# Unread products in TensorE's pauses, S5's last block in PSUM, and the place of the adaLN sums

## The chip, the cores and the metric

The kernel runs on one core of a Trainium2 chip. Five engines work side by side on the on-chip memory: TensorE (PE; its weight loads are shown apart as PEld), VectorE (DVE), ScalarE (ACT), GpSimd (POOL) and SyncE (SP), which here only issues transfers. TensorE writes into PSUM, from which the other engines read. The metric is the device time of one execution in microseconds; lower is better.

## The reference, cut to what matters

Four layers work on 256 latent and 256 context tokens of width 1024. Layer i mixes tokens by its kind (0 pooling, 1 a bidirectional S5 state-space layer with a GLU, 2 neighbourhood attention, 3 pooling again), and a gated ConvFFN follows each.

```python
for i in range(DEPTH):
    mod_lat = (cond_lat @ ada_w[i] + ada_b[i])[:, None, :]
    sh1, sc1, g1, sh2, sc2, g2 = jnp.split(mod_lat, 6, axis=-1)
    u_lat = _modulate(_rmsnorm(h_lat, norm1_g[i]), sh1, sc1)
    ...
    h_lat = h_lat + g1 * y_lat
    v_lat = _modulate(_rmsnorm(h_lat, norm2_g[i]), sh2, sc2)
    h_lat = h_lat + g2 * _conv_ffn(v_lat, ffn_w_up[i], ffn_conv_w[i], ffn_conv_b[i], ffn_w_down[i])
```

The context stream goes through the same steps with the same weights as long as a later layer reads it. In S5 each group of 16 channels drives 64 complex states in both directions:

```python
a_bar, b_bar = _s5_discretise(a_re[direction], a_im[direction], log_dt[direction], ...)
h_lat = _diag_scan(a_bar, bu, reverse)
y_lat.append(jnp.real(jnp.einsum('blgp,gcp->blgc', h_lat, c_cplx)))
# glu_out: g = gelu(y + d_skip * u); (g @ w1 + b1) * sigmoid(g @ w2 + b2)
```

## The kernel before, in words

**Products.** A large product is made of three: weights and data are each split into a high and a low part (`whi`, `wlo`; `uh`, `ul` or `ah`, `al` or `gh`, `gl`), and `mm3` adds high x high, low x high and high x low in PSUM. SP fetches a raw block of weights, ACT makes `whi` (L58), VectorE `wlo` (L159), some blocks ahead (`ahead`, `prep_hi`, `prep_lo`, `_prep`; `prep_parts` yields between the pieces of one block). Engines take their instructions in the order in which the program issues them: this order is written by hand, and waits follow from tiles and buffers.

**Norms.** `rstd` adds up the squares of all channels by products with ones (the tile `ssq`; the last channel's squares, `sq_last`, come latest), makes the inverse root on ACT and VectorE (`rsqrt`, tile `rs`) and spreads it over 128 partitions by one product with `sel` for each group of tokens (the tile `rstd`). Then `split_mod` makes q = h x gs x rstd on VectorE, `uh` on ACT and `ul` on VectorE, channel block by channel block; `up` uses them.

**PSUM.** Eight banks: four with the tag `up` (pool `psu`), two `acc` (`psa`), two others.

**ConvFFN.** `ffn(l, ...)` goes over 11 blocks f of hidden channels: `up(half, weights, k)` for k in 0 to 7, the convolution of width 3 and the gate (VectorE and ACT, tile `t`, then `ah`, `al`), and in parts the products `dn` down to the residual stream. In block 0 the two halves run interleaved, the second `lag` steps behind the first. Ahead of ConvFFN 0, `start` has already split two channel blocks and issued the turning products of S5's tables (`s5_fat`, tiles `s5fat`, copied by ACT to `s5ft`).

**adaLN.** The modulation vectors of the next layers are summed beside the ConvFFNs (`ada_vec`). Each job is (layer, first chunk, chunks, letters): "V" multiplies and adds on VectorE in one pass of 128x2048 (L55), "P" multiplies on ACT and adds on POOL (L321), "M" does the first two as "V" and the others as "P".

**S5.** Eight blocks m of channels. `v_mm` makes v in PSUM, `scan` turns v by a decaying phase (VectorE, three passes), scans it along the tokens into an SBUF tile g (`tensor_tensor_scan`), and turns back: y1 = g x cos and y2 = g (parts swapped) x sin, two passes of 128x1024 (L1530, L1531), on POOL except that the last block's y2 is on VectorE. `join` adds y2 to y1 (L1535; VectorE, for two blocks POOL). `z_mm` makes the output of a block: 32 products with the short kernel k and 64 products with c, of 64 rows each, that read y. In the last pass of the loop, m = 7, `z_mm(6)` is issued, and behind the loop `join(7)` and `z_mm(7)`; then the GLU's products follow.

## Time and profile before

| what | value |
|---|---|
| time, median of 3 runs | 1741.68 us (1740.31 to 1742.18) |
| the profiled execution's own time | 1745.49 us |
| its span | 1743.7 us |
| mean granted clock of TensorE | 0.963 of full speed |
| TensorE busy | 1642.7 us (94%) |
| VectorE busy | 1317.5 us (76%) |
| ScalarE busy | 785.2 us (45%) |
| GpSimd busy | 382.2 us (22%) |

Busy time is the time in which an engine had an instruction in work; the granted clock is what TensorE was given, 1.0 for 2.4 GHz and 0.5 for 1.2 GHz. All times that are given as points ("at 592.1") are microseconds from the span's start.

### The profile page before, as it was taken

The numbers are of one execution on the slowest core, as the hardware profiler recorded it, in microseconds if no ns is written. First come the engines' busy times: TensorE is split into PE (matmuls) and PEld (weight loads), VectorE is DVE, ScalarE is ACT, GpSimd is POOL, SyncE is SP. The second block draws the span as 40 slices with busy tenths as digits, with TensorE's granted clock in tenths as the row PEclk, the third lists the DMA queues.
The fourth block names the chain that finished last, engine by engine and source line by source line (L and its number), as shares of the span: only waits on it lengthen the run. The fifth ranks groups of instructions, "written<-read, shape, count | busy, mean of one in ns | idle before, by whom it ended". The sixth has DMA issues, their size and how long they took to land.

```text
span 1743.7 us, 26649 instructions
## 1 busy us (share of the span) xinstructions
PE 1642.7 (94%) x10482; PEld 1359.1 (78%) x10482; DVE 1317.5 (76%) x2007; ACT 785.2 (45%) x1236; POOL 382.2 (22%) x317
## 2 busy tenths in 40 slices
PE   7899999999987898899999989999999999999998
PEld 4467778777767886787878867787778999889997
DVE  6768868799749758687878688726658989678876
ACT  4533314223263242544232543436666466575553
POOL 0015355565618501000000340201220000111001
PEclk9989999999998699899999999999999999999999
DMA  9669798786869843342646555233227866545553
GB/s 381 269 201 251 246 311 261 213 236 184 252 194 391 308 169 145 138 152 104 234 175 233 203 212 191 93 119 130 95 91 253 289 212 213 213 169 174 190 181 110
DMA packets 98181, 356.88 MB, mean 205 GB/s; under 512 B 14296, under 2 KB 37368, under 8 KB 72200
## 3 DMA queue, kind: packets, MB, share of 16 engines
q1 hardware_dynamic: 93400, 334.09, 56.8%
q0 software_dynamic: 4080, 18.99, 3.0%
q8 instruction: 83, 1.36, 0.3%
q10 hardware_dynamic: 576, 2.10, 0.3%
q14 instruction: 42, 0.34, 0.1%
HBM read 324.19 MB, written 30.94 MB: 204 GB/s over the span
## 4 chain that ended last, share of the span: by engine, by line
PE 59%; DVE 17%; DMA 5%; issue 4%; ACT 4%; POOL 3%; SPq 1%; DVEq 0%; ACTq 0%; POOLq 0%
PE p L61 28%; PE dn L61 14%; DVE wlo L159 5%; PE glu L61 4%; DMA s5fl<-s5dA 4%; DVE t L55 3%; PE v L61 2%; PE k L61 2%; PE wo L61 1%; ACT whi L58 1%; PE q L61 1%; DVE s5bt L1328 1%; DVE s5vt L1327 1%; DVE h L55 1%; PE z L61 1%
## 5 line engine op out<-in xcount | busy, mean ns | idle before, releaser
L61 PE MATMUL p<-uh,whi 128*128 128x512 f32 (+1 forms) x1408 | 482.1, 342 | 17.0 <-DVE t L55 8.2
L61 PE MATMUL p<-uh,wlo 128*128 128x512 f32 (+1 forms) x1408 | 480.2, 341 | 4.7 <-DVE wlo L159 2.8
L61 PE MATMUL p<-ul,whi 128*128 128x512 f32 (+1 forms) x1408 | 480.4, 341 | 0.6 <-DVE ul L55 0.4
L159 DVE TENSOR_TENSOR wlo<-raw,whi 128x1024 fp32r<-128x1024 f32 x334 | 378.2, 1174 | 118.6 <-ACT whi L58 117.4
L58 ACT ACTIVATE whi<-raw 128x1024 fp32r<-128x1024 f32 x352 | 318.3, 952 | 260.1 <-PE dn L61 71.7
L61 PEld LDWEIGHTS p<-uh,whi 128*128 128x128 f32 x1408 | 270.0, 192 | 58.9 <-issue 16.0
L61 PEld LDWEIGHTS p<-uh,wlo 128*128 128x128 f32 x1408 | 269.9, 192 | 36.2 <-DVE wlo L159 4.5
L61 PEld LDWEIGHTS p<-ul,whi 128*128 128x128 f32 x1408 | 269.8, 192 | 31.6 <-DVE ul L55 1.7
L61 PE MATMUL dn<-ah,wlo 128*128 128x512 f32 (+1 forms) x704 | 239.9, 341 | 9.7 <-DVE wlo L159 9.7
L61 PE MATMUL dn<-ah,whi 128*128 128x512 f32 (+1 forms) x704 | 242.0, 344 | 5.4 <-ACT whi L58 2.9
L61 PE MATMUL dn<-al,whi 128*128 128x512 f32 (+1 forms) x704 | 239.0, 340 | 2.6 <-DVE al L819 2.6
L55 DVE SCALAR_TENSOR_TENSOR t<-p,conv_sb,t 128x510 f32<-128x510 f32 (+1 forms) x352 | 208.2, 612 | 25.6 <-ACT t L58 19.3
L61 PEld LDWEIGHTS dn<-ah,whi 128*128 128x128 f32 x704 | 135.0, 192 | 29.3 <-issue 10.6
L61 PEld LDWEIGHTS dn<-ah,wlo 128*128 128x128 f32 x704 | 134.8, 191 | 27.3 <-DVE wlo L159 12.1
L61 PEld LDWEIGHTS dn<-al,whi 128*128 128x128 f32 x704 | 134.8, 191 | 17.2 <-DVE al L819 3.1
L55 DVE SCALAR_TENSOR_TENSOR ads<-ada,cT_sb,ads 128x2048 f32<-128x2048 f32 (+1 forms) x69 | 140.5, 2066 | 6.6 <-DMA ada<-in_ada_dram 5.0
L58 ACT ACTIVATE t<-p,conv_sb 128x512 f32<-128x512 f32 (+1 forms) x176 | 107.6, 661 | 53.7 <-PE p L61 53.6
L321 POOL TENSOR_TENSOR ads<-ads,ada 128x2048 f32<-128x2048 f32 (+1 forms) x11 | 45.6, 4157 | 345.1 <-ACT ada L58 334.5
L55 DVE SCALAR_TENSOR_TENSOR h<-dn,mods,h 128x256 f32<-128x256 f32 x192 | 83.8, 477 | 39.8 <-PE dn L61 39.6
L58 ACT ACTIVATE t<-t 128x512 f32<-128x512 f32 (+1 forms) x88 | 45.9, 522 | 149.6 <-DVE t L55 141.0
L58 ACT ACTIVATE ah<-t 128x512 fp32r<-128x512 f32 (+1 forms) x88 | 46.0, 523 | 141.9 <-DVE t L810 132.1
L1316 POOL TENSOR_TENSOR s5ct<-s5bc,s5pw 128x512 f32<-128x512 f32 x32 | 42.7, 1333 | 223.1 <-DMA s5bc<-in_s5c_dram 146.4
(256 smaller groups left out, 2300.2 us busy)
## 6 DMA issues: line engine op xcount, KB each, us to landing
raw<-in_wup_dram SPq DMA_DIRECT2D x88, 1024.0 KB, 5.2
ada<-in_ada_dram SPq DMA_DIRECT2D x84, 1024.0 KB, 7.6
raw<-in_wdn_dram SPq DMA_DIRECT2D x32, 768.0 KB, 4.3
raw<-in_wdn_dram SPq DMA_DIRECT2D x32, 640.0 KB, 4.0
raw<-in_qkv_dram SPq DMA_DIRECT2D x12, 1024.0 KB, 4.9
ada<-in_ada_dram POOLq DMA_DIRECT2D x12, 1024.0 KB, 5.4
s5bt<-in_s5bT_dram SPq DMA_DIRECT2D x32, 256.0 KB, 6.6
s5fl<-s5dA SPq DMA_DIRECT2D x32, 256.0 KB, 7.4
```

Of the source, the lines that this page charges most:

```text
L55: return self.nc.vector.scalar_tensor_tensor(out, in0, scalar, in1, op0=op0, op1=op1, **kw)
L58: return self.nc.scalar.activation(out, in_, func, **kw)
L61: return self.nc.tensor.matmul(out, lhsT, rhs, start=start, stop=stop)
L159: self.nc.vector.tensor_sub(lo[:, s], t[:, s], hi[:, s].bitcast(F32))
L321: self.nc.gpsimd.tensor_add(y, y, t)
L1316: G.tensor_tensor(ct[:, o], *x, op=ALU.mult)
L1327: V.tensor_mul(tv, bT[:, :, ::-1], fa[:, :, 1:2].to_broadcast([P, 2, 2, 128]))
L1328: V.tensor_mul(ba, bT, fa[:, :, 0:1].to_broadcast([P, 2, 2, 128]))
```

## The change

- A new function `keep(n)` issues n fp32 products of the identity with 256 columns of `sel` into a PSUM tile of tag `up` that nobody reads. `rstd` calls it at three places: ahead of the sums of the last squares (only where `ssq` was begun early), ahead of the inverse root's use, and after the broadcast. The numbers are (1, 4, 6) in S5, (4, 3, 3) in ConvFFN 1, (1, 3, 1) in attention, (1, 3, 2) in ConvFFN 2 and in pool layer 3, (0, 3, 2) in ConvFFN 3. `start` ends with five, S5's loop has eight in its last pass: 56 in all.
- S5's last block: the scan writes over v in PSUM, and VectorE makes y2, then v x cos in place, then y1 = sum, six passes of 128x512 in all; POOL's pass and `join(7)` go. `z_mm(7)` is issued behind the eight products and ahead of `z_mm(6)`.
- ConvFFN 0: the low parts of its first weight block are issued ahead of the second channel block's split, the preparation of the next block ahead of the last splits, and the lag is 3 instead of 4.
- The sums of (2, 8, 4) in ConvFFN 1 go from "P" to "V", those of (3, 10, 2) ahead of ConvFFN 3 from "M" to "V".

```diff
@@ -609,11 +609,13 @@
         next(t)
         next(fat[3])
         uh, ul = self.new_u()
-        self.split_mod(0, 1, LC, r, uh, ul, range(2))
+        self.split_mod(0, 1, LC, r, uh, ul, range(1))
+        next(parts)
+        next(parts)
+        self.split_mod(0, 1, LC, r, uh, ul, range(1, 2))
         for g in fat[2:]:
             next(g)
-        next(parts)
-        next(parts)
+        self.keep(5)
         self.pre = r, uh, ul, parts
 
     def mod(self, l, ch, c, d):
@@ -702,7 +704,14 @@
         self.nc.vector.tensor_copy(rc, pc)
         return rc
 
-    def rstd(self, bank=0, also=lambda: None, apart=False):
+    def keep(self, n):
+
+        if n:
+            ps = self.psu.tile([P, 512], F32, tag="up", name="keep")
+            for _ in range(n):
+                self.mm(ps[:, :2 * P], self.eye, self.sel[:, :2].rearrange("p j n -> p (j n)"), True, True)
+
+    def rstd(self, bank=0, also=lambda: None, apart=False, keep=(0, 0, 0)):
         n = self.tok().stop - self.tok().start
         ng = n // P
         ps, self.ssq = self.ssq, None
@@ -711,19 +720,23 @@
             self.sq_eps(ps)
             for j in range(ng):
                 self.mm(ps[32 * j:32 * j + 32, :P], self.ones, self.sq_acc[:, j * P:(j + 1) * P], False, False)
+            self.keep(keep[0])
             for j in range(ng):
                 self.mm(ps[32 * j:32 * j + 32, :P], self.ones, self.sq_last[:, j * P:(j + 1) * P], False, True)
         np_ = 32 * ng
+        self.keep(keep[1])
         x = self.rsqrt(ps, np_)
         also()
         if apart:
             rs = [self.psa.tile([P, T], F32, tag="acc", name="rstd"), self.bank("rstd", [P, T], bank)]
             for j in range(ng):
                 self.mm(rs[j // 2][:, j % 2 * P:(j % 2 + 1) * P], self.sel[:np_, j], x, True, True)
+            self.keep(keep[2])
             return lambda c: rs[c]
         rb = self.rb_all = self.bank("rstd", i=bank)
         for j in range(ng):
             self.mm(rb[:, j * P:(j + 1) * P], self.sel[:np_, j], x, True, True)
+        self.keep(keep[2])
         base = self.tok().start
         return lambda c: rb[:, c * T - base:(c + 1) * T - base]
 
@@ -768,7 +781,7 @@
         if len(conds) == 1:
             self.third = ap_, self.n_prep + 1, self.n_use + NF + 16
         if l:
-            r = self.r or self.rstd(apart=full)
+            r = self.r or self.rstd(apart=full, keep=(4, 3, 3) if full else (1, 3, 2))
             self.r = None
             if self.n_prep == self.n_use:
                 self._prep()
@@ -837,7 +850,7 @@
             self.ada_ahead()
             if f == 0:
 
-                lag = (4, 8, 3, 3)[l]
+                lag = (3, 8, 3, 3)[l]
                 ws = [self.take()]
                 for k in range(KD + lag):
                     if k < KD:
@@ -848,6 +861,8 @@
                         for ds in {0: ((2, 4), (4, 6), (6, KD)), 1: ((2, KD),)}.get(l, ((2, 3), (3, 6), (6, KD))):
                             self.split_mod(l, 1, conds, r, uh, ul, range(*ds))
                             next(parts, None)
+                            if l == 0 and ds[0] == 2:
+                                self._prep()
                         next(parts, None)
                         ws.append(self.take())
                         if not full:
@@ -1451,7 +1466,7 @@
             nc.gpsimd.memset(ys[i][0][:, 0:1], 0.0)
 
         signs = [self.s5us[:, 1024 * i:1024 * i + 1024].rearrange("p (d s n) -> p d s n", d=2, s=2) for i in range(2)]
-        r = self.rstd()
+        r = self.rstd(keep=(1, 4, 6))
 
         rs = pp.tile([P, 2, 32], F32, tag="rs", name="rs")
         v = self.tp.tile([P, 2, 32, 8], F32, tag="t", name="rsm", bufs=3)
@@ -1511,7 +1526,7 @@
 
             cs = self.s5tab.pop(("r", m))[:, 0][:, :, None].to_broadcast([P, 2, 2, 256])
             sn = signs[m % 2]
-            g = pp.tile([P, 2, 2, 256], F32, tag="g", name="g", bufs=2)
+            g = pp.tile([P, 2, 2, 256], F32, tag="g", name="g", bufs=2) if m < KD - 1 else None
             vs = [v.rearrange("p c j n -> p c (j n)") for v in vps.pop(m)]
             xs = []
             for v, d in zip(vs, range(2)):
@@ -1523,12 +1538,21 @@
             for v, x in zip(vs, xs):
                 V.tensor_add(v, v, x)
             for v, d in zip(vs, range(2)):
-                V.tensor_tensor_scan(g[:, d].rearrange("p c n -> p (c n)"), rts[m % 2][d].rearrange("p c j n -> p (c j n)"),
+                V.tensor_tensor_scan((g[:, d] if m < KD - 1 else v).rearrange("p c n -> p (c n)"), rts[m % 2][d].rearrange("p c j n -> p (c j n)"),
                                      v.rearrange("p c n -> p (c n)"), 0.0, ALU.mult, ALU.add)
 
             y1, y2 = (y.rearrange("p (d c n) -> p d c n", d=2, c=2) for y in (ys[m % 2][0][:, 1:1025], ys[m % 2][1]))
-            nc.gpsimd.tensor_mul(y1, g, cs)
-            (V if m == KD - 1 else nc.gpsimd).tensor_mul(y2, g[:, :, ::-1], sn[:, :, ::-1])
+            if m < KD - 1:
+                nc.gpsimd.tensor_mul(y1, g, cs)
+                nc.gpsimd.tensor_mul(y2, g[:, :, ::-1], sn[:, :, ::-1])
+                return
+
+            for v, d in zip(vs, range(2)):
+                V.tensor_mul(y2[:, d], v[:, ::-1], sn[:, d, ::-1])
+            for v, d in zip(vs, range(2)):
+                V.tensor_mul(v, v, cs[:, d])
+            for v, d in zip(vs, range(2)):
+                V.tensor_add(y1[:, d], v, y2[:, d])
 
         def join(m, eng):
             y = ys[m % 2][0][:, 1:1025]
@@ -1665,6 +1689,9 @@
                 self._fill_dma()
             if m == KD - 1:
                 split_hi(1)
+            if m == KD - 1:
+                self.keep(8)
+                z_mm(m)
             if m:
                 step("z", m - 1, z_mm)
             if m in (2, 4, 6):
@@ -1674,8 +1701,6 @@
                 self.limit = self.n_dma + 1
                 self._fill_dma()
                 self.prep_hi()
-        join(KD - 1, V)
-        z_mm(KD - 1)
         back(3)
         self.limit = len(self.blocks)
         self._fill_dma()
@@ -1723,7 +1748,7 @@
         LC = (0, 1)
         es = ExitStack()
         pp = es.enter_context(self.tc.tile_pool(name="nat", bufs=1))
-        r = self.rstd(apart=True)
+        r = self.rstd(apart=True, keep=(1, 3, 1))
         uh, ul = self.new_u()
         parts = self.prep_parts()
         for ds in ((0, 3), (3, 5), (5, 7), (7, 8)):
@@ -2018,7 +2043,7 @@
             if self.stop == 10:
                 return self.dump()
             self.ffn(1, LC, self.after_ffn(LC), [(1, 10, 2, "VV"), (2, 0, 4, "VV"), (2, 4, 4, "V"),
-                                                   (2, 8, 4, "P"), (3, 0, 4, "V")])
+                                                   (2, 8, 4, "V"), (3, 0, 4, "V")])
             self.finish()
             if self.stop == 11:
                 return self.dump()
@@ -2029,11 +2054,11 @@
                 if d == 0:
                     self.pool_w(3, pm)
                     self.pool_win(pm)
-                    self.ada_init([(3, 10, 2, "M")], 1, (self.up_, self.u_bufs, 0, 2))
+                    self.ada_init([(3, 10, 2, "V")], 1, (self.up_, self.u_bufs, 0, 2))
                     self.ada_ahead()
 
             self.ffn(2, LO, self.after_ffn(LO, pool_in), [(3, 4, 4, "V"), (3, 8, 2, "V")])
-            r = self.rstd()
+            r = self.rstd(keep=(1, 3, 2))
             us = self.pool_u(3, LO, r)
             self.sq_pe_start(LO)
             self._prep()
@@ -2043,7 +2068,7 @@
                 next(self.ada_gen)
             self.pool_y(LO, pm, range(KD))
             self.ada_steps = [2, 6, 0, 0]
-            self.r = self.rstd()
+            self.r = self.rstd(keep=(0, 3, 2))
             self.ffn(3, LO, self.after_ffn(LO), None)
             self.final()
```

## Rows read from the trace of the kernel before

**Rows 1.** The page: the chain that ended last, by engine

```profile
PE 59%; DVE 17%; DMA 5%; issue 4%; ACT 4%; POOL 3%; SPq 1%; DVEq 0%; ACTq 0%; POOLq 0%
```

**Rows 2.** Windows: length, busy PE, PEld, DVE, ACT, POOL, then clock, DMA share, GB/s

```profile
575.00:580.10 5.10, 5.02 (x96) 4.75 (x96) 4.65 (x7) 0.26 (x1) 5.08 (x3) 1.00 0.98 323
582.00:616.50 34.50, 31.14 (x297) 29.40 (x298) 21.30 (x19) 10.08 (x20) 10.06 (x6) 0.51 0.63 252
720.00:726.00 6.00, 5.62 (x13) 4.25 (x14) 5.63 (x15) 4.33 (x9) 0.00 (x0) 0.52 0.00 0
978.00:1026.00 48.00, 43.69 (x193) 35.04 (x191) 37.82 (x38) 29.34 (x31) 28.14 (x6) 1.00 0.49 164
1026.00:1033.00 7.00, 5.16 (x12) 4.09 (x13) 7.00 (x4) 1.86 (x3) 6.13 (x2) 0.51 0.44 150
1109.00:1114.00 5.00, 2.73 (x33) 1.57 (x32) 3.81 (x8) 1.44 (x4) 3.99 (x13) 1.00 0.37 106
1520.20:1524.75 4.55, 4.51 (x11) 3.67 (x12) 2.98 (x7) 4.55 (x9) 0.00 (x0) 0.53 0.00 0
1524.75:1529.50 4.75, 4.75 (x24) 4.18 (x24) 3.57 (x6) 3.76 (x6) 0.00 (x0) 1.00 0.46 140
```

**Rows 3.** Timeline of PE at pool layer 3: start, length, idle before

```profile
1520.24 9.26 PE L61 MATMUL pz<-pw,pu 128*128 128x256 f32 x32 [1.12 <-ACT pu L58]
```

**Rows 4.** Timeline of PE and ACT at ConvFFN 0's beginning

```profile
86.61 0.79 PE L61 MATMUL p<-uh,wlo 128*128 128x512 f32 x1 [1.80 <-DVE wlo L176]
...
98.18 0.80 PE L61 MATMUL p<-uh,whi 128*128 128x512 f32 x1 [2.89 <-ACT whi L58]
...
84.81 2.40 ACT L58 ACTIVATE s5ft<-s5fat 32x512 f32<-32x512 f32 x4
```

**Rows 5.** Timeline of PE at S5's norm

```profile
522.94 1.13 PE L61 MATMUL rstd<-rs,sel_sb 128*128 128x128 f32 x8 [2.11 <-DVE rs L55]
527.16 5.77 PE L61 MATMUL v<-U,s5b 128*64 128x64 f32 x128 [3.09 <-DVE U L1477]
...
549.88 2.09 PE L61 MATMUL v<-U,s5b 128*64 128x64 f32 x64
```

**Rows 6.** Timelines of PE and DVE at S5's end

```profile
576.27 3.79 PE L61 MATMUL z<-y,s5c 64*128 64x64 f32 x64
...
585.01 7.09 PE L61 MATMUL z<-y,s5c 64*128 64x64 f32 x64
...
612.54 0.79 PE L61 MATMUL glu<-gh,whi 128*128 128x512 f32 x1
...
582.95 1.29 DVE L1522 TENSOR_TENSOR v<-v,s5r 128x512 f32<-128x512 f32 x2
...
587.76 4.86 DVE L1531 TENSOR_TENSOR y<-g,us 128x1024 f32<-128x1024 f32 x1
592.55 4.52 DVE L1535 TENSOR_TENSOR y<-y,y 128x1024 f32<-128x1024 f32 x2
```

**Rows 7.** Timeline of PE at the norm of ConvFFN 1

```profile
717.19 2.07 PE L61 MATMUL rstd<-rs,sel_sb 128*128 128x128 f32 x8 [1.35 <-DVE rs L55]
```

**Rows 8.** ConvFFN 1 from 978 to 1046: lines (POOL), timelines of DVE and PE

```profile
L321 POOL TENSOR_TENSOR ads<-ads,ada 128x2048 f32<-128x2048 f32 x7 | 34.3, 4896 | 286.5 <-ACT ada L58 286.2
...
1009.34 4.34 DVE L819 TENSOR_TENSOR al<-t,ah 128x512 fp32r<-128x512 f32 x1 [0.70 <-ACT ah L58]
...
1020.19 0.69 DVE L819 TENSOR_TENSOR al<-t,ah 128x512 fp32r<-128x512 f32 x1 [0.70 <-ACT ah L58]
...
1023.03 9.46 DVE L159 TENSOR_TENSOR wlo<-raw,whi 128x1024 fp32r<-128x1024 f32 x2 [1.36 <-ACT whi L58]
...
1039.90 2.35 DVE L55 SCALAR_TENSOR_TENSOR ads<-ada,cT_sb,ads 128x2048 f32<-128x2048 f32 x1 [2.10 <-DMA ada<-in_ada_dram]
...
1027.85 0.79 PE L61 MATMUL dn<-ah,wlo 128*128 128x512 f32 x1 [4.06 <-DVE wlo L159]
```

**Rows 9.** Timeline of PE at the norm of ConvFFN 3

```profile
1542.67 0.58 PE L61 MATMUL p<-uh,whi 128*128 128x256 f32 x1 [1.11 <-ACT uh L58]
```

## The prediction

> **What bounds the kernel now.** I read the page first: the chain that ended last is mostly TensorE (59%), then VectorE (17%), DMA only 5% [rows 1]. So time comes out where TensorE waits, or where it runs at its lower clock. The page's line of granted clock in 40 slices is near full everywhere; so what half clock (1.2 instead of 2.4 GHz) there is lies in short stretches, and I cut windows around them [rows 2]: the end of S5 (34.5 us at 0.51), the norms ahead of each ConvFFN (720 to 726 at 0.52), the pool layer's first products (0.53), and a hole in ConvFFN 1 (1026 to 1033 at 0.51). Each follows a pause of TensorE. Twice the work in the same stretch is what full clock would give: 11 matmul records in 4.55 us before the clock rose at 1524.75, 24 in 4.75 us after it.
>
> **Price of an unread product.** It is a plain fp32 product, 128x128 by 256 columns, as the pool layer's pz: 16 in the code, 32 records, 9.26 us [rows 3]. By the two windows a product (two records) costs 0.83 at half clock and 0.40 at full. 56 are added; where a pause holds them they cost nothing, where it doesn't they stand ahead of the next real product.
>
> **S5's norm (1, 4, 6 products).** The broadcast of rstd comes after a pause of 2.11 us, the first v products after 3.09 [rows 5]; four products need 1.6, six 2.4: both fit. Today 128 v products take 5.77; 64 take 2.09 at full clock, so 128 take 4.2: gain 1.5. Behind them the stretch hangs on transfers and POOL's passes, so it may be nothing: 0 to 1.6.
>
> **S5's end.** Block z(4) runs at full clock (1.00 from 575 to 580.1): its 64 c products take 3.79; those of z(5) to z(7) 7.09 each [rows 2, 6]. With the k products a block takes 5.1 or 9.1. TensorE pauses 3 us ahead of z(5) and its clock is down to 616.5, though it is then nearly always busy: 64-row products at half clock did not bring it up. Full 128-row fp32 products did, 4.5 us after their start [rows 2, 3]. Now the last block's y passes go to VectorE with the scan in place in PSUM. Today VectorE's y pass takes 4.86 beside POOL's and the two joins 4.52; the 128x512 passes on a PSUM operand take 1.29 for two [rows 6]. Six of these from the end of the scan (587.7) are 3.9: y(7) is there at 591.5, ahead of z(5)'s end at 592.1. SBUF – State Buffer, section Who interferes with whom, in the Trainium skill says that a VectorE instruction contends with GpSimd only where two of its inputs are in SBUF; by that rule the six stay at 0.65, and if they were slowed as the y pass is they would end some 5 us later, 4 us behind z(5), still under the eight unread products. Those start at 592.1, cold: 4.5 to 5.2 us until the clock rises, the rest at 0.40, 6.0 in all. Then z(7) 5.1, 0.5 for the turn-over, z(6) 5.1: the GLU starts at 608.8 instead of 612.5 [rows 6], and at full clock: its first 4.1 us at 0.51 are worth 2.0. Gain 3.7 + 2.0 = 5.7 (4.9 to 6.5). If the clock does not rise: 592.1 + 6.7 + 9.1 + 0.5 + 9.1 = 617.5, 5 us lost.
>
> **ConvFFN 0's order.** TensorE waits 1.80 us for the first wlo and 2.89 for block 1's whi; ACT's four s5ft copies take 2.40 between the first uh [rows 4]. Block 0's wlo now goes ahead of the second column's split, block 1's preparation ahead of the last splits; the lag drops from 4 to 3. That takes some 1.3 off the first wait and most of the second. But the first block's second PSUM tile now stands in the bank that the s5ft copies free, and these come later on ACT; VectorE's last ul is behind the new wlo; and the five unread products (2.0 to 4.2) stand ahead of the first real one. What follows hangs on a chain through a transfer and POOL's table passes. Worked through by the bank's release I get 0.5 of gain; between -2 (all unread products exposed) and 2.5 (most of both waits).
>
> **Norm of ConvFFN 1 (4, 3, 3).** The rstd broadcast takes 2.07 where the same eight take 1.13 at S5's norm at full clock [rows 5, 7]: 0.9. The next 5.6 us of TensorE's work, at 0.52 [rows 2], would be 2.8 shorter, but VectorE's splits then set the pace: by my estimate 0.8 of that stays. The pauses are 2.2, 1.35 and 1.1 us against 1.6, 1.2 and 1.2 of products at full clock. Gain 1.7 (1 to 2.6).
>
> **Layer 2's adaLN sums, POOL to VectorE, in ConvFFN 1.** Seven passes of 128x2048 take POOL 34.3 us, 4.9 each; on VectorE such a pass takes 2.35, so 16.4 are added there [rows 8]. While POOL runs, VectorE's own two-input passes stretch: al is 4.34 beside POOL, 0.69 without; a pair of wlo 9.46 against some 2.35 elsewhere. Over the stretch I count 18 us of such stretching, about what is added: VectorE has no more to do. But the stretching falls where TensorE waits: three waits between 1014 and 1028, of 0.6, 1.5 and 4.06 (the longest stands in [rows 8]), and after it 5.2 us of TensorE's work at a clock of 0.51 [rows 2], worth 2.6. Waits and clock together are 8.8. I put the new passes into VectorE's order by hand and find 0.3 us of stall that stay ahead of al: 8.5 (5 to 9.5; 3 if VectorE becomes the bound).
>
> **The other norms.** NAT (1, 3, 1): the clock is 1.00 throughout [rows 2]; one product delays the last sum of squares by 0.4: a loss of 0.4. ConvFFN 2 (1, 3, 2): its first products follow a pause of 1.11 us (those of ConvFFN 3 too; one of the two rows stands in [rows 9]) and run some 2.7 us cold, worth 1.3 at most; VectorE sets the pace soon after: 0.5 (0 to 1.3). Pool layer 3 (1, 3, 2): 4.55 us at 0.53 are worth 2.1, ACT's passes take part of it: 1.3 (1.0 to 2.8, with the broadcast's own half clock). ConvFFN 3 (0, 3, 2) runs cold for some 6 us, worth 3 at most; VectorE's splits go on for 2 us behind that, so some 1.2 remain; its four adaLN sums of half size go to VectorE too, 4 x 1.2 added against some 6 of stretching: 1.3. Together 2.5 (1.5 to 3.5).
>
> **Sum.** 0.5 + 1.5 + 5.7 + 1.7 + 8.5 - 0.4 + 0.5 + 1.3 + 2.5 = 21.8 us. The profiled execution took 1745.5 us, 3.8 over the median of the runs: 1723.7 by its time, 1741.7 - 21.8 = 1720 by the median.
>
> **The rivals.**
> (a) The eight products don't bring the clock up at S5's end, or it falls again in the 64-row blocks. For it: z(5) to z(7) stayed at half clock while busy. Against: z(4) held full clock in the same products. The 5.7 turn into 5 lost: 1731; half-way (it falls in z(6)) 1725.
> (b) VectorE becomes the bound in ConvFFN 1: it was busy 37.8 of 48 us from 978 to 1026 [rows 2], and sums in front of al or wlo delay TensorE in POOL's stead. 3 instead of 8.5: 1725.5. Against: the stretching that goes equals what is added.
> (c) The gains at S5's norm and ConvFFN 0 vanish under transfers and POOL: 2 less, 1722.
> (d) Slower: unread products neither raise nor hold the clock. They then cost 0.83 each and overrun the pauses: 3.1 at S5's norm (ten products, 8.3, in 5.2 of pause), 2.6 in ConvFFN 1, 1.7 in each of three small norms, 5 at S5's end, 4 in ConvFFN 0, about 20 lost against 10 won by the adaLN sums: 1752 at worst, 1748 if ConvFFN 0 hides its own. It decides where the granted clock stays at 0.5 under them. Against: pz, the same product, brought the clock from 0.53 to 1.00. TensorE: Matmul & The Clock Gate, Part 4: PE-mode transpose, in the Trainium skill says that transposes by an identity do not count as busy for the clock; the unread products have the identity as one operand, and should that rule hold for them this rival follows; no trace here shows it, since they are not in transpose mode.
>
> **How the numbers follow.** The forecast as summed has 0.70, with its own range of 1714 to 1726 by the parts' bounds; (a) 0.12, (b) 0.08, (c) 0.05 (inside that range), (d) 0.04; 0.01 for anything else. From 1713 to 1731 takes in (b), (c) and (a), and leaves out (d) and the sum of all upper bounds. A measurement here can tell about 0.2%, 3.5 us: faster 0.93, same 0.03 (a part of (a) with (b)), slower 0.04.
>
> **What the profile would show.** Clock at 1.00 in the v products after S5's norm and in 720 to 726; at S5's end a group of eight products, then z at 3.79 for its 64 c products, with the GLU some 4 us earlier after the same z(5); no POOL adaLN passes, al at 0.69 everywhere and no wait of over 1 us for wlo in ConvFFN 1. Wrong would be: z still at 7.09 (a); new waits for wlo or ah on VectorE at adaLN passes (b); keep products of 0.83 that end after the value that they waited with (d).

## The result, and the profile after

The changed kernel takes 1718.46 us in the median of four runs (1713.78 to 1722.19) against 1741.93 us (1740.31 to 1742.93) before: a ratio of 0.9864, 95% interval 0.9849 to 0.9879, faster by 23.5 us, or 1.4%. The forecast was 1720 (1713 to 1731). The profiled execution took 1713.78 us, the fastest of the four; a second profile is of an execution of 1723.8 us. The two together show more than either, so both are read below, as are two of before (1745.5 and 1742.8 us).

The page of the first profile, to set beside [rows 1]: the span, the granted clock in 40 slices, the chain that ended last.

```profile
span 1711.9 us, 26847 instructions
...
PEclk9999999999998999999999999999999999999999
...
PE 68%; DVE 15%; ACT 5%; DMA 4%; issue 3%; SPq 1%; POOL 1%; DVEq 0%; ACTq 0%; POOLq 0%
```

TensorE's share of the chain rose from 59 to 68%, the mean clock from 0.963 to 0.986 (0.979 in the second profile). Windows of the first profile, with the columns of [rows 2]: S5's end, the GLU's beginning, the first products of ConvFFN 1, its adaLN stretch, pool layer 3.

```profile
572.00:597.00 25.00, 24.07 (x428) 22.61 (x424) 17.16 (x23) 8.35 (x16) 11.55 (x7) 0.99 0.98 374
597.00:601.00 4.00, 4.00 (x21) 3.26 (x20) 1.56 (x2) 3.32 (x6) 0.00 (x0) 1.00 0.86 236
702.50:708.50 6.00, 5.23 (x21) 3.33 (x19) 5.63 (x15) 4.12 (x9) 0.00 (x0) 1.00 0.00 0
958.00:1012.00 54.00, 53.76 (x243) 43.02 (x242) 48.20 (x57) 21.66 (x30) 0.00 (x0) 1.00 0.61 202
1492.30:1499.30 7.00, 6.99 (x32) 6.12 (x33) 5.08 (x11) 7.00 (x13) 0.00 (x0) 1.00 0.00 1
```

All the stretches that were at 0.51 to 0.53 in [rows 2] are at 0.99 or 1.00 in this profile. In ConvFFN 1 from 978 to 1026 before, TensorE was busy 43.7 of 48 us; here it is 53.8 of 54.

Where the time went, by stretches of TensorE's timeline (start of the first product of one to that of the next, worked out from the four traces; "norm" is the first `ssq` product, "end" the end of the last product):

| stretch | before | before, 2nd | changed | changed, 2nd |
|---|---|---|---|---|
| ConvFFN 0's first p to S5's norm | 435.8 | 430.8 | 429.1 | 433.7 |
| S5's norm to z(5) | 64.1 | 65.5 | 66.3 | 65.7 |
| z(5) to GLU | 29.5 | 29.7 | 18.9 | 24.4 |
| GLU to ConvFFN 1's first p | 107.8 | 108.6 | 105.5 | 106.2 |
| that p to attention's v | 393.8 | 394.0 | 384.3 | 384.3 |
| v to ConvFFN 2's first p | 201.9 | 201.7 | 201.9 | 201.9 |
| that p to pool layer 3's pz | 204.2 | 204.5 | 203.6 | 203.8 |
| pz to ConvFFN 3's first p | 22.4 | 22.6 | 20.7 | 20.7 |
| that p to the end | 194.1 | 194.0 | 192.0 | 192.0 |

From ConvFFN 1 on each stretch repeats within 0.3 us in these four, so its difference can be read off: 9.6, 0, 0.7, 1.8 and 2.1 us. (The 0.7 is the least certain: in other profiles with the same ConvFFN 2 that stretch takes 203.4 to 204.5.) A norm lies at the end of the stretch ahead of its first product. Ahead of S5's norm and at S5's end the executions of one kernel differ by 4 to 6 us. These two places are what the experiments are about.

S5's end in the first profile, TensorE's timeline beside [rows 6], and VectorE's passes of the last block:

```profile
572.94 1.10 PE L61 MATMUL z<-U,s5k 128*64 128x64 f32 x32
573.97 3.79 PE L61 MATMUL z<-y,s5c 64*128 64x64 f32 x64
578.22 1.31 PE L61 MATMUL z<-U,s5k 128*64 128x64 f32 x32 [0.47 <-ACT G L58]
579.46 3.79 PE L61 MATMUL z<-y,s5c 64*128 64x64 f32 x64
583.18 3.72 PE L61 MATMUL keep<-sel_sb,eye_sb 128*128 128x256 f32 x16
586.83 1.15 PE L61 MATMUL z<-U,s5k 128*64 128x64 f32 x32
...
597.12 0.50 PE L61 MATMUL glu<-gh,whi 128*128 128x512 f32 x1
```

```profile
581.69 1.27 DVE L1551 TENSOR_TENSOR y<-v,us 128x512 f32<-128x512 f32 x2
582.87 1.29 DVE L1553 TENSOR_TENSOR v<-v,s5r 128x512 f32<-128x512 f32 x2
584.07 1.28 DVE L1555 TENSOR_TENSOR y<-v,y 128x512 f32<-128x512 f32 x2
585.69 1.23 DVE L1559 TENSOR_TENSOR y<-y,y 128x1024 f32<-128x1024 f32 x1 [0.34 <-POOL y L1547]
```

The pause ahead of z(5) is 0.47 us, z(5) runs at full clock, the eight products take 3.7 us. The six passes take 3.7 us from 581.69 to 585.35, though POOL runs its own two passes beside them (580.95 to 585.65): some 0.6 each, as forecast. Each of the six has one input in PSUM. By the section Who interferes with whom of SBUF – State Buffer in the Trainium skill, a VectorE instruction contends with GpSimd where two of its inputs are in SBUF or where it runs in a two-port mode, which such two-input passes do not have; these rows agree with that. The second profile has another S5 end:

```profile
575.15 3.79 PE L61 MATMUL z<-y,s5c 64*128 64x64 f32 x64
581.94 2.03 PE L61 MATMUL z<-U,s5k 128*64 128x64 f32 x32 [3.00 <-ACT G L58]
583.90 7.09 PE L61 MATMUL z<-y,s5c 64*128 64x64 f32 x64
590.93 5.21 PE L61 MATMUL keep<-sel_sb,eye_sb 128*128 128x256 f32 x16
596.06 1.15 PE L61 MATMUL z<-U,s5k 128*64 128x64 f32 x32
597.14 3.79 PE L61 MATMUL z<-y,s5c 64*128 64x64 f32 x64
```

```profile
590.19 0.69 DVE L1555 TENSOR_TENSOR y<-v,y 128x512 f32<-128x512 f32 x1 [1.25 <-PE z L61]
591.07 0.69 DVE L1555 TENSOR_TENSOR y<-v,y 128x512 f32<-128x512 f32 x1 [0.19 <-PE z L61]
```

Here the pause is 3.00 us and z(5) is at half clock, as in [rows 6]. Under the eight products the clock comes up (5.21 us for 16 records, between 3.7 at full and 6.7 at half clock), and z(7) has 3.79. This is the picture that the prediction drew, but for one wait: VectorE's last sum waits for z(5), which still reads the buffer that y(7) is written to. So y(7) is there at 591.8, behind z(5)'s end at 591.0 and not ahead of it; the eight products still cover that. Products of the identity did raise the clock, then (the run without them, below, stayed at half clock): the rule on transposes in TensorE: Matmul & The Clock Gate, Part 4, of the Trainium skill does not reach them.

### The profile page after: what moved, and what is told of

It is laid out like the page before. It is cut to its first block, busy times and chain, and to the rows that moved or that the text cites. A ratio compares the mean times of both kernels' runs of the same rounds, so it can differ in the third digit from the quotient of the medians.

```text
span 1711.9 us, 26847 instructions
## 1 busy us (share of the span) xinstructions
PE 1639.3 (96%) x10594; PEld 1351.9 (79%) x10594; DVE 1302.1 (76%) x2022; ACT 768.0 (45%) x1225; POOL 333.6 (19%) x305
## 4 chain that ended last, share of the span: by engine, by line
PE 68%; DVE 15%; ACT 5%; DMA 4%; issue 3%; SPq 1%; POOL 1%; DVEq 0%; ACTq 0%; POOLq 0%
PE p L61 32%; PE dn L61 17%; DVE wlo L159 4%; PE glu L61 4%; PE v L61 3%; PE z L61 2%; DVE t L55 2%; DVE ads L55 2%; PE k L61 2%; DMA s5fl<-s5dA 2%; PE wo L61 1%; PE adp L61 1%; ACT whi L58 1%; PE o L61 1%; PE q L61 1%
## 5 line engine op out<-in xcount | busy, mean ns | idle before, releaser
L61 PE MATMUL p<-uh,whi 128*128 128x512 f32 (+1 forms) x1408 | 478.2, 340 | 10.1 <-DVE t L55 8.5
L61 PE MATMUL p<-uh,wlo 128*128 128x512 f32 (+1 forms) x1408 | 474.9, 337 | 2.8 <-DVE wlo L159 2.1
L159 DVE TENSOR_TENSOR wlo<-raw,whi 128x1024 fp32r<-128x1024 f32 x334 | 368.2, 1144 | 106.5 <-ACT whi L58 105.2
L61 PEld LDWEIGHTS p<-uh,whi 128*128 128x128 f32 x1408 | 266.2, 189 | 53.3 <-issue 18.0
L61 PEld LDWEIGHTS p<-ul,whi 128*128 128x128 f32 x1408 | 266.3, 189 | 40.0 <-DVE ul L55 11.8
L61 PEld LDWEIGHTS p<-uh,wlo 128*128 128x128 f32 x1408 | 266.1, 189 | 32.1 <-DVE wlo L159 2.6
L55 DVE SCALAR_TENSOR_TENSOR t<-p,conv_sb,t 128x510 f32<-128x510 f32 (+1 forms) x352 | 208.0, 612 | 20.6 <-ACT t L58 14.4
L55 DVE SCALAR_TENSOR_TENSOR ads<-ada,cT_sb,ads 128x2048 f32<-128x2048 f32 (+1 forms) x80 | 161.9, 2052 | 10.7 <-DMA ada<-in_ada_dram 10.2
L645 POOL TENSOR_TENSOR sqa<-sq 128x512 f32<-128x512 f32 (+1 forms) x6 | 7.5, 1246 | 685.3 <-PE adp L61 368.9
```

The lines of the kernel that those rows point to most:

```text
L55: return self.nc.vector.scalar_tensor_tensor(out, in0, scalar, in1, op0=op0, op1=op1, **kw)
L61: return self.nc.tensor.matmul(out, lhsT, rhs, start=start, stop=stop)
L159: self.nc.vector.tensor_sub(lo[:, s], t[:, s], hi[:, s].bitcast(F32))
L645: self.nc.gpsimd.tensor_add(self.sq_sum[:, :n], self.sq_acc[:, :n], q[:, :n])
```

## The experiments

Ratios are to the kernel before, run on the same chip. Not all runs were on one chip, so small differences between them are read from the ratios and not from the times.

**The changed kernel again** (no edit).

> The changed kernel once more, unaltered. Its four runs lay at 1713.8, 1715.8, 1721.1 and 1722.2 us. Theory: two kinds of execution that part ahead of S5's block z(5). Where TensorE comes late to z(4), the pause ahead of z(5) closes (0.47 us in the first profile, 2.99 before) and the clock stays up: z(5) takes 5.0 and the eight unread products 3.7. Where it comes early, the pause is some 2.5 to 3 us, z(5) takes 9.1 and the eight products about 6: 6 to 7 us more. So a profile near 1721 shows the c products of z(5) at 7.09, one near 1715 at 3.79. Rival: the spread comes from ahead of S5 (waits on transfers for the tables between 130 and 520 us), and z(5) is alike in both; then the two profiles differ by several us at S5's norm already.

Median 1717.27 us (1715.72 to 1723.8), ratio 0.9871 (0.9852 to 0.989). The profiled execution was the slowest, 1723.8, and shows z(5) at 7.09 as above. Of its 10 us over the first profile 5.5 lie between z(5) and the GLU (24.4 against 18.9), 4.3 ahead of S5's norm. Theory and rival each account for about half.

**Before again** (no edit).

> The kernel before once more, unaltered, for a second profile. Between the two profiles of the changed kernel S5's norm lay 4.3 us apart (511.9 and 516.2) and z(5)'s start 3.7; in the first profile of before they stood at 518.9 and 583.1. Theory: the stretch ahead of S5 varies by some 4 us from execution to execution in both kernels, and S5's middle gives part of it back, so the norm lies between 515 and 519 here; z(5) at half clock in any case. Rival: before stands still at 518.9 within 1 us, and the 3 to 8 us that all five profiles since have gained there come from the change in ConvFFN 0.

Median 1742.12 us (1740.02 to 1746.85), ratio 0.9999 (0.9984 to 1.0014). S5's norm at 513.5, 5.5 us earlier than in the first profile of before, with the old ConvFFN 0: a bit further than expected, and the rival falls. Its z blocks, on TensorE's timeline and VectorE's, show something that the first profile hid:

```profile
578.97 1.31 PE L61 MATMUL z<-U,s5k 128*64 128x64 f32 x32 [0.80 <-ACT G L58]
580.21 3.79 PE L61 MATMUL z<-y,s5c 64*128 64x64 f32 x64
584.47 1.31 PE L61 MATMUL z<-U,s5k 128*64 128x64 f32 x32 [0.47 <-ACT G L58]
592.12 7.09 PE L61 MATMUL z<-y,s5c 64*128 64x64 f32 x64 [6.34 <-DVE y L1535]
```

```profile
583.68 7.24 DVE L1531 TENSOR_TENSOR y<-g,us 128x1024 f32<-128x1024 f32 x1
590.85 2.35 DVE L1535 TENSOR_TENSOR y<-y,y 128x1024 f32<-128x1024 f32 x2
```

z(5) is at full clock here too, against what was expected, and it gained nothing: z(6) then waited 6.34 us for join(6), which stood on VectorE behind a y pass of 7.24 us beside POOL, and the clock fell there. From z(5) to the GLU it is 29.7 us, as with z(5) at half clock (29.5). In this execution VectorE's y pass and join(6) set S5's end. In the first profile of before z(5) came out of its pause at half clock, and z(6) waited for join(6) even so:

```profile
583.05 2.03 PE L61 MATMUL z<-U,s5k 128*64 128x64 f32 x32 [2.99 <-ACT G L58]
...
595.99 7.09 PE L61 MATMUL z<-y,s5c 64*128 64x64 f32 x64 [1.38 <-DVE y L1535]
```

Over all profiles, z(5) to the GLU is 28.0 to 30.3 us in the four with S5's end as before, whatever z(5)'s clock, and 18.8 to 24.4 in the eight with the changed end and its eight products.

**S5's end as before.** The scan into g, POOL's y1 and VectorE's y2 of the last block, and this order:

```diff
-            if m == KD - 1:
-                self.keep(8)
-                z_mm(m)
             if m:
                 step("z", m - 1, z_mm)
...
+        join(KD - 1, V)
+        z_mm(KD - 1)
         back(3)
```

> The changed kernel with S5's end as before (POOL's and VectorE's passes of the last block, z(6) ahead of z(7), no eight unread products). By the prediction's term 5.7 us more than the changed kernel. By the first profile after, where z(5) too ran at full clock, 10.6 us from z(5)'s start to the GLU's and 2 more in the GLU: 12 to 13 more where it holds, 6 where it does not; mean some 8 to 10. The end of S5 at half clock again: the GLU starts some 29 us after z(5).

1728.26 us (1725.95 to 1732.08), ratio 0.993 (0.9915 to 0.9945): 11 us more than the changed kernel on this chip. z(5) to the GLU 28.0 us, z(5) to z(7) at 7.09. Nearly twice the prediction's 5.7 by the medians; by the profiles' stretches it is 6.3 up to the GLU (28.0 against the mean of 18.9 and 24.4) and 1.2 in the GLU.

**No unread products at S5's end**, scan in PSUM and order kept; run twice.

```diff
             if m == KD - 1:
-                self.keep(8)
                 z_mm(m)
```

> The changed kernel without the eight unread products at S5's end, scan in PSUM and the order z(7), z(6) kept. If the new order alone closes the pauses, nothing is lost where z(5) ran at full clock: z(7) follows when y(7) is there, and it gains up to the 1 to 2 us that the products run past y(7). If the products are what brings the clock up, then where z(5) is at half clock z(7) and z(6) are too, 9.1 each instead of 5.1, and the GLU's first 4 us at half clock: 8 + 2 - 5.2 = 5 us more. By the theory of two kinds: 5 more in the executions with a pause ahead of z(5), 1 to 2 less in the others. The prediction's own term: 5.7 minus what order alone brings (612.5 less 592.1 + 18.7 = 610.8, 1.7), 4 us more.

1726.06 us (1717.31 to 1730.02), ratio 0.9901 (0.988 to 0.9921), but the profiled execution was the one of 1717.31: z(5), z(7) and z(6) all at full clock, 16.8 us from z(5) to the GLU, 2 less than with the products. The other five took 1724.68 to 1730.02.

> The changed kernel without the eight unread products at S5's end, a second time, for a profile of an execution near its median: its profiled execution took 1717.3 us with z(5) to z(6) at full clock and lost nothing, the other five took 1724.7 to 1730.0. Theory: in those the clock falls in a pause ahead of z(5) (2 to 3 us) or ahead of z(7), nothing brings it up, z(7) and z(6) take 9.1 each and the GLU's first 4 us run at half clock; from z(5)'s start to the GLU's then 27 to 28 us, as with S5's end of before, against 16.8 in the first profile. Rival: those executions lose their 8 us ahead of S5's norm, which then lies near 520.

1724.75 us in the profiled execution (1727.89 in the other one), ratio 0.9914 (0.9881 to 0.9946). TensorE's timeline:

```profile
578.49 1.37 PE L61 MATMUL z<-U,s5k 128*64 128x64 f32 x32 [1.57 <-ACT G L58]
579.79 7.09 PE L61 MATMUL z<-y,s5c 64*128 64x64 f32 x64
587.35 2.04 PE L61 MATMUL z<-U,s5k 128*64 128x64 f32 x32 [0.47 <-ACT G L58]
589.32 7.09 PE L61 MATMUL z<-y,s5c 64*128 64x64 f32 x64
596.88 2.04 PE L61 MATMUL z<-U,s5k 128*64 128x64 f32 x32 [0.47 <-ACT G L58]
598.84 7.09 PE L61 MATMUL z<-y,s5c 64*128 64x64 f32 x64
605.87 0.79 PE L61 MATMUL glu<-gh,whi 128*128 128x512 f32 x1
```

A pause of 1.57 us ahead of z(5), and nothing brings the clock up until the GLU: 27.4 us from z(5) to the GLU, as expected, with S5's norm at 513.1 and not near 520. The eight products are an insurance: the clock may fall ahead of z(5) or not. Where it falls they save 3 us up to the GLU (24.4 against 27.4) and some 1.2 in it, where it doesn't they cost 2. The scan in PSUM without the products is this run; the products without the scan in PSUM were not tried.

**Six more products ahead of z(5).**

```diff
+            if m == KD - 2:
+                self.keep(6)
             if m:
                 step("z", m - 1, z_mm)
```

> The changed kernel with six more unread products ahead of z(5), for the pause there. Theory: they hold the clock through a pause of 3 us, so every execution is of the faster kind: z(5) 5.0 instead of 9.1 and the eight products 3.7 instead of 5.2, 5.5 us less in the executions near 1721 to 1724, up to 2 us more in those near 1714 to 1716 (where the pause was 0.5 and the products stand in the way); the spread of the runs shrinks, median 1 to 3 us less. Rival: the kinds are not of z(5) but of the stretch ahead of S5, and the median stays or grows by up to 2.4.

1716.18 us (1715.23 to 1723.2), ratio 0.9858 (0.9837 to 0.9879). In its profile the six took 2.86 us and closed the pause, z(5) was at full clock and 18.8 us lay between z(5) and the GLU. But one run still took 1723.2, and where it lost its 8 us was not seen. By the ratios 1 to 2 us better than the changed kernel, which these runs can't tell from nothing.

**ConvFFN 0's order as before.**

```diff
-        self.split_mod(0, 1, LC, r, uh, ul, range(1))
-        next(parts)
-        next(parts)
-        self.split_mod(0, 1, LC, r, uh, ul, range(1, 2))
+        self.split_mod(0, 1, LC, r, uh, ul, range(2))
         for g in fat[2:]:
             next(g)
-        self.keep(5)
+        next(parts)
+        next(parts)
...
-                lag = (3, 8, 3, 3)[l]
+                lag = (4, 8, 3, 3)[l]
...
-                            if l == 0 and ds[0] == 2:
-                                self._prep()
```

> The changed kernel with ConvFFN 0's order as before (no unread products there, low parts and preparation later, lag 4). The prediction's term is 0.5 with bounds -2 to 2.5: 0.5 us more than the changed kernel. Rival by the profiles since: S5's norm starts 2.7 to 8 us earlier in all five kernels with the new order, so its removal costs 3 to 6 us, as far as S5's middle does not take it back (there 1.6 to 3.2 us have been lost since).

1717.47 us (1714.58 to 1720.54), ratio 0.986 (0.9839 to 0.9881): no difference. S5's norm stood at 509.7, the earliest of all profiles, with the old order. The rival falls; the stretch ahead of S5 varies by itself (what varies in it is told at the end of the next section).

**No unread products at the norms.** All five `keep=` arguments of `rstd` go; they serve six norms, since `ffn`'s stands for ConvFFN 1 and 2.

> The changed kernel without the unread products at the five norms; those at ConvFFN 0 and at S5's end stay. By the prediction's terms (1.5 at S5's norm, 1.7, -0.4, 0.5, 1.3 and 1.2 of the 2.5 at ConvFFN 3) it takes 5.8 us more than the changed kernel, about 1724. Rival: S5's norm brings nothing, since transfers set its pace afterwards, and the others are eaten by VectorE's splits: 0 to 3 us more. Clock after each norm 0.5 again, v products of S5's first two blocks 5.8 instead of 3.95.

1728.94 us (1721.89 to 1731.66), ratio 0.9926 (0.9907 to 0.9944): 11 us more, above both expectations. Its stretches from the GLU on hold 2.8 (GLU to ConvFFN 1; 0.9 of it is that norm, most of the rest the GLU at half clock, since z(6) fell to 7.09 in this execution), 0.2, 0.2, 0.9, 1.3 and 0.9 us, 6.3 in all. Attention's norm, at full clock in [rows 2], came out at half clock here: its rstd broadcast took 1.96. It fell in the kernel before with the adaLN sums alone, too (5.6 us from its first `ssq` to v, 5.1 before).

**No unread products at S5's norm alone.** `keep=(1, 4, 6)` goes.

> The changed kernel without the 1, 4 and 6 unread products at S5's norm alone. Without all of those at the norms the median was 11 us higher, but of that the profile's stretches outside S5 hold only 6.5 us (2.8 from the GLU to ConvFFN 1, 0.9 + 1.3 + 0.9 behind, 0.6 in attention). Theory A: the other 4 to 5 us are S5's: the cold v products at its norm bring TensorE early or late to the pauses at S5's end, so it takes 4 to 5 us more than the changed kernel here. Theory B (the prediction's): at most 1.5 more, as a stretch that hangs on transfers follows; then the rest of the 11 was the spread of the executions.

1719.91 us (1717.05 to 1723.99), ratio 0.9866 (0.9846 to 0.9886): not to be told from the changed kernel's 0.9864 and 0.9871. (The median lies 2.6 above that of the changed kernel on another chip, where before was faster too, 1740.35 against 1743.27.) The stretch from S5's norm to z(5) is 66.2 us, 66.3 and 65.7 with the products. Theory A is not borne out by the profile; what makes up the rest of the 11 us above stays open.

**Unread products of 64 rows at the norms.**

```diff
-                self.mm(ps[:, :2 * P], self.eye, self.sel[:, :2].rearrange("p j n -> p (j n)"), True, True)
+                self.mm(ps[:, :2 * P], self.eye[:rows], self.sel[:rows, :2].rearrange("p j n -> p (j n)"), True, True)
```

> The changed kernel with the unread products at the norms cut to 64 of the 128 rows of the identity and of sel (same number, same 256 columns, same time each). Theory: rows decide: at S5's end 96 products of 64 and 128 rows with 64 columns ran for 27 us at half clock without bringing it up, and 128-row products did within 5 us; then the clock is at 0.5 after the norms, as without the products, and it takes 6 to 11 us more than the changed kernel. Rival: it is the columns or the share of busy time, not the rows: clock 1.00 after the norms and no time lost.

1720.6 us (1717.85 to 1723.77), ratio 0.9874 (0.9859 to 0.9889). By the ratio no time is lost. The clock is 1.00 after five of the six norms, ConvFFN 1's among them, against the theory. But behind ConvFFN 2's norm it fell. Windows over the norm and over the first products behind it, this run first, then the first profile of the changed kernel:

```profile
1287.40:1292.20 4.80, 4.55 (x30) 2.96 (x29) 3.38 (x8) 2.22 (x5) 1.17 (x2) 1.00 0.65 225
1292.20:1297.00 4.80, 4.67 (x22) 4.17 (x23) 4.80 (x11) 3.22 (x6) 0.00 (x0) 0.64 1.00 423
...
1283.90:1288.80 4.90, 4.84 (x30) 3.10 (x29) 3.40 (x8) 2.23 (x5) 1.17 (x2) 1.00 0.67 231
1288.80:1293.60 4.80, 3.67 (x26) 3.26 (x27) 4.80 (x11) 3.23 (x6) 0.00 (x0) 1.00 0.98 416
```

0.64 is what the kernel before has there, too (1316.0 to 1320.8). In all nine profiles with products of 128 rows at this norm the clock stays at 1.00. So neither the theory nor its rival holds everywhere: 64 rows were enough at five norms and not at the sixth, in one profile. Whether 64 rows can raise a clock that is down was not tried; the eight products at S5's end kept their 128.

**The adaLN sums on POOL again, in the changed kernel.**

```diff
-(2, 8, 4, "V"), (3, 0, 4, "V")
+(2, 8, 4, "P"), (3, 0, 4, "V")
...
-self.ada_init([(3, 10, 2, "V")]
+self.ada_init([(3, 10, 2, "M")]
```

> The changed kernel with both adaLN changes undone (the sums of layer 2 in ConvFFN 1 and of layer 3 ahead of ConvFFN 3 on POOL again). By the prediction 8.5 + 1.3 = 9.8 us more than the changed kernel; by the first profile after 8.9 from 971 to 1037 and about 1 behind: the same. The rival, that VectorE as bound keeps most of the gain down, would give 3 to 4. The waits for wlo of 0.6, 1.5 and 4.1 us come back.

1731.05 us (1724.99 to 1734.33), ratio 0.9948 (0.9933 to 0.9963): 13.8 more; in its profile, 8.3 in ConvFFN 1 and 0.9 behind ConvFFN 3's norm. The three waits of ConvFFN 1 came back with 0.58, 1.48 and 4.07 us; the second is for ACT's whi, the others for wlo. The profile is of the fastest of the six runs, and what makes up the rest of the 13.8 stays open.

**The adaLN sums alone, in the kernel before** (the reverse of that diff).

> The kernel before with both adaLN changes alone. By the prediction 8.5 + 1.3 = 9.8 us less than before, by the profile's stretches 8.3 + 0.9 = 9.2; taking them out of the changed kernel cost 13.7 in the median. If the parts simply add, it is 9 to 10 less than before (ratio 0.9945); if the sums on VectorE are worth more among the other parts, under 9 less here.

1734.51 us (1730.39 to 1736.21) against 1743.27 on the same chip, ratio 0.995 (0.9936 to 0.9964): 8.8 less; in its profile 9.4 in ConvFFN 1 and 1.0 behind. The parts add within what the runs can tell.

Taken out of the changed kernel one at a time, S5's end, the products at the norms and the adaLN sums cost 11, 11 and 13.8 us by the medians, half as much again as the whole change gave. The stretches of the same runs' profiles hold 7.5, 6.3 and 9.2, 23 in all. Each of these profiles is of one of the two fastest runs of its kernel; the excess of the medians is not explained.

## Why the prediction was right, and where not

The sum was right, 21.8 against 23.5, and the mechanism of each large part; the terms were less even than the sum. That the sum came so near is in part luck: S5's end gave some 3.5 us more than its term, and the norms together some 2.5 less than theirs.

- **AdaLN sums: 8.5 + 1.3.** Measured 8.3 to 9.4 and 0.9 to 1.0 by the stretches, 8.8 by the runs of the sums alone. The lines of ConvFFN 1 beside [rows 8], then VectorE's busy time in the whole stretch and the one wait for wlo that is left:

```profile
L55 DVE SCALAR_TENSOR_TENSOR ads<-ada,cT_sb,ads 128x2048 f32<-128x2048 f32 x7 | 16.4, 2346 | 0.1
...
L832 DVE TENSOR_TENSOR al<-t,ah 128x512 fp32r<-128x512 f32 x4 | 2.8, 692 | 2.8 <-ACT ah L58 2.8
```

Windows from ConvFFN 1's first p to attention's v, before and after, with the columns of [rows 2]:

```profile
720.38:1114.15 393.77, 384.98 (x1713) 307.36 (x1713) 308.70 (x363) 166.69 (x213) 45.38 (x25) 0.98 0.50 178
...
702.57:1086.89 384.32, 382.86 (x1724) 304.87 (x1723) 306.52 (x371) 153.57 (x206) 11.12 (x18) 1.00 0.51 182
```

The wait:

```profile
1002.88 0.50 PE L61 MATMUL dn<-ah,wlo 128*128 128x512 f32 x1 [0.24 <-DVE wlo L159]
```

  The seven passes cost VectorE 16.4 us, as worked out, and its own passes fell back: the four al of this stretch from 10.1 to 2.8 us in all. So VectorE is busy for 306.5 us of the stretch where it was busy for 308.7: it has no more to do, as forecast, and the three waits shrank to one of 0.24. Rival (b) did not come.
- **S5's end: 5.7, mis-sized.** Measured 8 from z(5) to the GLU (29.6 to 21.7 in the mean of two profiles each) and some 1.3 in the GLU, where 2.0 were forecast; taken out, 11 by the medians. The prediction had z(5) at half clock in every execution and the GLU 3.7 us earlier. In the second profile that is what happened (24.4 us against a forecast of 25.7), in the first z(5) kept its clock and it was 18.9. In the one profile of before that had z(5) at full clock this had been of no use, since z(6) waited for VectorE's join(6); the new passes took that wait away too. This is the step that was off: the term was sized from one execution, in which the join looked like work that ends beside a cold TensorE, and not like the bound that it is once z(5) is fast. Rival (a), that the clock falls again in the 64-row blocks, did not come in the two profiles of the changed kernel. It came in two others, both without products at S5's norm: z(6) at 7.09 behind pauses of 1.89 and 1.63 us. That the missing products made these pauses is not shown.
- **ConvFFN 0: 0.5.** Nothing measurable, as forecast. The new wait is there: the fourth channel block's ul comes behind the new wlo, and TensorE waits 3.33 us for it at 96.17, much as it waited 2.89 for whi [rows 4].
- **S5's norm: 1.5, not found.** The v products of the first two blocks take 3.95 us instead of 5.77, but then wait for transfers (rows of the first profile):

```profile
516.92 2.75 PE L61 MATMUL keep<-sel_sb,eye_sb 128*128 128x256 f32 x12
520.18 3.95 PE L61 MATMUL v<-U,s5b 128*64 128x64 f32 x128 [0.50 <-DVE U L1492]
527.96 3.57 PE L61 MATMUL v<-U,s5b 128*64 128x64 f32 x64 [3.83 <-DMA s5b<-s5dB]
```

  This is the lower bound of that term and rival (c).
- **The other norms: 1.7, -0.4, 0.5, 1.3, and 1.2 for ConvFFN 3.** The table has the time from a norm's first `ssq` to the first product behind it, then that of the 96 products that follow (unread ones not counted), in the first profile of before, in the changed kernel without products at the norms, and in its first profile:

| norm | before | without | changed |
|---|---|---|---|
| ConvFFN 1 | 8.4 + 24.7 | 8.3 + 24.4 | 7.4 + 24.6 |
| attention | 5.1 + 23.2 | 5.6 + 23.4 | 5.1 + 23.2 |
| ConvFFN 2 | 4.8 + 13.3 | 4.8 + 13.5 | 4.9 + 13.2 |
| pool layer 3 | 5.3 + 16.4 | 4.8 + 16.0 | 4.9 + 14.7 |
| ConvFFN 3 | 10.5 + 14.2 | 10.5 + 14.4 | 10.9 + 13.2 |

  ConvFFN 1's norm gave 0.9 to 1 ahead of its first p and next to nothing behind: the products wait on VectorE's ul at once (0.36 us). Attention's cost nothing against before; beside the adaLN sums on VectorE, where the clock fell without them, they are worth 0.6. ConvFFN 2's gave 0.2, pool layer 3's 1.2, ConvFFN 3's 0.7 to 0.8, though its first product came 0.4 later.
- **The price of a product** was 0.40 at full clock by pz, and eight products (16 records) take 3.72 us, 0.46 each; at S5's norm four take 1.99. In the pauses they hid but for the 0.4 at ConvFFN 3. Rival (d) is excluded by the clock in every window of the first profile above.

The executions differ by up to 9 us ahead of S5's norm (509.7 to 518.9 over the fourteen profiles), whatever the kernel. The prediction looked for half clock in the stretches of [rows 2]. But from ConvFFN 0's first p to that norm TensorE is idle for 18.3 to 24.7 us and at half clock for 13.7 to 34.1 us (34.1 in the first profile of before, 20.5 in that of the changed kernel). Take the idle time and half of the busy time at half clock off a stretch of 427.8 to 435.8 us, and 397.2 to 399.1 are left in all fourteen. So the spread lies in ConvFFN 0's pauses and the clock behind them, 30 us or more that this change hardly touches; what moves them from execution to execution stays open.

## What to carry to other kernels

Where two causes of delay lie on top of each other (an engine's clock and another engine's passes), taking one away can gain nothing, as z(5) at full clock did before: cost the wait that would be left. Work moved from GpSimd to a fuller VectorE can be free, if VectorE's own passes had been stretched beside GpSimd: compare the same instruction with and without company. And profile a second execution before a term is sized from one: 4 to 6 us here were the execution's and not the kernel's.

## What the runs showed of the hardware

- The clock of S5's z products, once at 0.5, stayed there from 579.8 to the GLU at 605.9, though TensorE paused for no more than 0.47 us at a time (7.09 for every c group, the second profile without the eight products). Eight unread products brought it to 1.00 within 5.2 us.
- Products that use 64 of 128 rows kept the clock at 1.00 through five norms, as those of 128 rows did, but not through ConvFFN 2's: 0.64 over the 4.8 us behind it, after 4.55 us of TensorE's work in 4.8, against 1.00 in nine profiles with 128 rows. What keeps the z products from raising the clock stays open.
- Pauses of nearly the same length ended both ways: z(5) came out at full clock behind 1.45 us of pause and at half clock behind 1.57.
- A VectorE pass of 128x1024 with two inputs in SBUF took 4.86 us in one execution and 7.24 in another of the same kernel. Both times it ended 1.1 us behind the last of POOL's passes that ran without a pause beside it (two of them, then three).
